# Two banks for the second layer's output columns of sample 0, and the products of the probabilities with v as bunches of eight

## The chip, the cores and the metric

The kernel runs on one core of a Trainium2 chip, as one program. The metric is the device time of one execution in microseconds; lower is better. TensorE (PE, with its weight loads PEld), VectorE (DVE), ScalarE (ACT), GpSimd (POOL) and the DMA queue on SyncE (SP) each work through their own list of instructions in order, and wait for one another through semaphores.

## The reference

A trunk of two layers is applied to two samples, each of 512 tokens by 1024 features, with the same weights. Layer 0 is RWKV-7 time mixing with a forward and a backward scan. Layer 1, where the change lies, is a two-dimensional neighbourhood attention over 8 rows by 64 columns of tokens, with 16 heads of 64 features, a gate and a projection; norms stand before and behind each layer:

```python
xn = _rms_norm(x, pre_norm_g[1])
proj = xn @ w_in + b_in
q, k, v, z = jnp.split(proj, 4, axis=-1)
o = _neighbourhood_attention(heads(q) * (HEAD_DIM ** -0.5), heads(k), heads(v), rpb)
h = (o.reshape(bsz, t, D_INNER) * jax.nn.silu(z)) @ w_o + b_o
x = x + _rms_norm(h, post_norm_g[1])
```

A query attends to all 8 rows and to a window of 16 columns. The scores get a bias and a mask, then a softmax, and the probabilities are multiplied with v.

## The kernel before

Activations lie with the features on the 128 partitions and the 512 tokens along the free dimension, so eight blocks k of 128 features make one sample. A projection column is one block p of 128 output features: 24 products of 128x128 by 128x512 into one PSUM bank, three for each k, since every fp32 operand is split into a high and a low part (`halves`, L375 the high, L376 the low) and high x high (L426), high x low (L427) and low x high (L428) are summed. The weights of a column come in two halves of 128x512, each loaded into `raw` (3 buffers) and split into `whi` and `wlo` (4 buffers each). The operands of a projection lie in pairs named `act` (18 buffers, nine pairs).

The first 1100 us are projections and scans whose order is written out by a planner; the change does not touch them. The rest of the program (`rest`) is written as interleaved generators: `run(g, (o, n))` takes n steps of o for each step of g. A scheduler then orders the instructions of each engine by its own estimate of times and by priorities: what stands under `high_priority(n)` is placed earlier where it can be. The stages of `rest` are:

- the last projections of sample 0 (`inproj(0)`) and the output projection of layer 0 for sample 1 (`out0(1)`), beside the attention of sample 0 (`heads(0, p)`, one call for each of the eight pairs of heads);
- the output columns of layer 1 for sample 0 (`out1(0)`), beside the normalisation of sample 1 between the layers (`norm0(1)`);
- the projections of sample 1 (`inproj(1)`, banks `pg`), beside the attention of sample 1 (`heads(1, p)`) and the transposes of `by_token`;
- the output projection of sample 1 (`last`).

In `heads`, a pair of heads is worked off in two half pairs of two column blocks n each, ns = (0, 1) and (2, 3). For a half pair come eight products q k into the bank `sc` (L1421, under priority SHP), then for each n the softmax on VectorE and ScalarE (L1430 to L1435), the transposes of the probabilities into `pt` (L1437), a copy to the factor `pts` (L1440), and after both n eight products with v into the bank `po` (L1450), four for each n: two parts e of the keys, two heads h, the heads on the two halves of the array's columns. At the end L1456 multiplies `po` with the gate into `oa`.

In `out1`, the operands are the eight `oa`, split by L375 and L376. Column p goes to the bank that OUT1[p % 4] names; ScalarE empties it at L1471 (out `os`) and squares it for the norm (L437, L440; sum L441). The bank `pm` is a single one, `pg` are two, which `inproj` and `out0` use in turn.

In `norm0`, after the sums of L452, a square root (L455), and the products of L464, the scale is copied out at L466. Then VectorE scales all eight blocks h (L1294), adds the loaded x (`xr`, 3 buffers, L1295), ScalarE squares (L1296, L1298) and VectorE sums (L1300). `x1n` makes the operands of `inproj(1)` from h (L1356 and L1357).

Of the kernel before, what the change touches and what calls it, by code (L numbers as in the profile page):

```python
# [234 lines left out]
class Trunk:  # L235
# [1 line left out]
    POST0, POST, POST2, POST3, NPA = 0.7, 1.0, 0.15, 0.66, 5  # L237
    HP, HS = (1000, 0), 1000
    SHP = 2000
    OUT1 = ("pm",) * 4  # L240
    LOW = 15
    LA = -40
    LATER = (0, 40, 0, 0)
# [1150 lines left out]
    def heads(self, s, p):  # L1394

        nc = self.nc
        vt, act, gps = nc.vector, nc.scalar, nc.gpsimd
        b = lambda tag, shape=(P, T), n=1, dt=F32: self.t(tag, shape, n, dt, self.ap)
        bias = b("bias", (P, 2, 3, 256), self.NBI)
        for h in range(2):  # L1400
            self.load(bias[:, h].rearrange("p a b -> p (a b)"), self.a["rpb"][2 * p + h])
        q, k, v = (self.load(b(kind, n=2), self.sp[kind, s, p]) for kind in ("q1", "k1", "v1"))
        yield
        vtok = b("vtok", (P, 7, P), self.NK)
        for j0, j1 in ((0, 4), (4, 7)):
            ps = self.p("pt", (P, 4, P))
            for j in range(j0, j1):
                nc.tensor.transpose(ps[:, j - j0], v[:, 64 * j:64 * j + P], self.ident)
            act.copy(vtok[:, j0:j1], ps[:, 0:j1 - j0])
            yield  # L1410
        op = self.p("po", (P, 4, P))
        cols = (0, 8, 24, 32)
        for ns in ((0, 1), (2, 3)):

            sc = self.p("sc", (P, 2, 2, 256))
            with self.tc.high_priority(self.SHP):
                for n in ns:
                    for a in (0, 64):
                        for h in range(2):
                            hs = slice(64 * h, 64 * h + 64)  # L1420
                            nc.tensor.matmul(  # L1421
                                sc[a:a + 64, h, n % 2], q[hs, n * P + a:n * P + a + 64], k[hs, 8 * cols[n]:8 * cols[n] + 256],
                                start=True, stop=True)
            pts = []
            for n in ns:
                pt = self.p("pt", (P, 2, 2, P))
                for h in range(2):
                    sb = b("sb", (P, 256), self.NSB)
                    mx = b("mx", (P, 4), 6)
                    vt.tensor_tensor_reduce(  # L1430
                        sb, sc[:, h, n % 2], bias[:, h, (0, 1, 1, 2)[n]], 1.0, -3.0e38, op0=ALU.add, op1=ALU.max, accum_out=mx[:, 0:1])
                    vt.tensor_scalar(mx[:, 1:2], mx[:, 0:1], -1.0, None, op0=ALU.mult)  # L1432
                    act.activation(sb, sb, AF.Exp, bias=mx[:, 1:2], accum_out=mx[:, 2:3])  # L1433
                    vt.reciprocal(mx[:, 3:4], mx[:, 2:3])
                    vt.tensor_scalar(sb, sb, mx[:, 3:4], None, op0=ALU.mult)  # L1435
                    for e in range(2):
                        nc.tensor.transpose(pt[:, h, e], sb[:, e * P:(e + 1) * P], self.ident)  # L1437
                    yield
                pts.append(b("pts", (P, 2, 2, P), self.NPT))
                act.copy(pts[-1], pt)  # L1440
                if n % 2 == 0:
                    yield
            if ns[1] == 3:
                while ("z1", s, p) not in self.sp:
                    yield
                z = self.load(b("z1"), self.sp["z1", s, p])
            for n in ns:
                for e in range(2):
                    for h in range(2):
                        nc.tensor.matmul(  # L1450
                            op[64 * h:64 * h + 64, n], vtok[:, cols[n] // 8 + 2 * e, 64 * h:64 * h + 64], pts[n % 2][:, h, e],
                            start=(e == 0), stop=(e == 1))
            yield
        with self.tc.high_priority(self.HP[s] if p == NP - 1 else 0):
            o = self.tmp() if s else self.t("oa", (P, T), NP, F32, self.ap)
            vt.tensor_tensor(o, op.rearrange("p n t -> p (n t)"), z, op=ALU.mult)  # L1456
            if s:
                lo, hi = (self.t("os", (P, T), 2 * NP, F32R, self.ap) for _ in range(2))
                o = self.halves(o, lo, hi)
        self.os[s].append(o)  # L1460
        yield

    def out1(self, s):
# [4 lines left out]
        for p in range(NP):  # L1468
            ps = yield from self.gemm(self.weight(self.a["w_ao"][p]), x, self.OUT1[p % 4])
            h = self.t("os", (P, T), 2 * NP, F32R, self.ap).bitcast(F32)  # L1470
# [419 lines left out]
```

## Time and profile before

| | |
|---|---|
| median of 3 runs | 1702.96 us (1696.2 to 1705.31) |
| profiled execution | 1697.02 us, its span 1695.2 us |
| mean granted TensorE clock in it | 0.959 |
| busy: PE, PEld | 1547.8 us (91%), 1178.6 us (70%) |
| busy: DVE, ACT | 1198.9 us (71%), 983.1 us (58%) |
| products with v (L1450) | 512 records, 1175.7 to 1655.5 us |
| scores (L1421) | 512 records, 1112.3 to 1629.5 us |
| eviction of an output column (L1471) | 8, median 682 ns, 1336.8 to 1394.6 us |

A row of a timeline reads: start, duration, engine, line, operation, out<-in, kind of tile, shape, count, and in brackets the idle time of the engine just before it and what ended that. Matmuls overlap in the array, so the distance between two starts is what a product costs, not its duration. A fp32 product with v or for scores has two records each. Times are from the span's start.

### The profile page before, as it was taken

The page shows a single profiled execution, that of the slowest core. Times are in us where ns is not written, and L with a number is a line of the kernel's source. Part 1 is how long each engine was busy: PE and PEld are TensorE (multiplying, and loading weights), DVE is VectorE, ACT ScalarE, POOL GpSimd, SP SyncE. Part 2 cuts the span into 40 slices and gives each one's busy share as a digit, 9 for nine tenths or more (in the row PEclk, how much of TensorE's full clock was granted, in tenths as well). Part 3 has the DMA queues.
Part 4 walks back from the last instruction along what each step waited for, and adds up shares of the span by engine and source line. Part 5 has one row for each costly group of instructions (what it writes and reads, how often), then busy time and mean ns, then how long its engine had stood idle before and what let it go on. Part 6 is the DMA issues. An engine that isn't in the chain of part 4 may idle for free.

```text
span 1695.2 us, 46252 instructions
## 1 busy us (share of the span) xinstructions
PE 1547.8 (91%) x18880; PEld 1178.6 (70%) x18880; DVE 1198.9 (71%) x2645; ACT 983.1 (58%) x2001; POOL 20.6 (1%) x64
## 2 busy tenths in 40 slices
PE   7989877987989898898899989999999889999997
PEld 6766655765756676676677767778777677777776
DVE  8986788777897888777798984534566746555564
ACT  5444665657767585567756545434566654555562
POOL 0000000000000000000000000000000000000000
PEclk9989888998998999899999999999999899999999
DMA  5435786778675777868674665464564237555553
GB/s 207 162 125 194 230 287 196 215 219 253 215 239 179 221 233 251 233 195 240 216 227 156 228 203 183 151 240 153 179 223 132 87 101 245 190 160 182 162 174 100
DMA packets 237365, 329.98 MB, mean 195 GB/s; under 512 B 53312, under 2 KB 118976, under 8 KB 237152
## 3 DMA queue, kind: packets, MB, share of 16 engines
q1 hardware_dynamic: 237152, 327.01, 60.7%
q8 instruction: 149, 2.44, 0.6%
q14 instruction: 64, 0.52, 0.1%
HBM read 223.52 MB, written 103.42 MB: 193 GB/s over the span
## 4 chain that ended last, share of the span: by engine, by line
PE 49%; DVE 9%; ACT 8%; DMA 6%; issue 3%; SPq 0%; DVEq 0%; ACTq 0%
PE pg L426 5%; PE pg L427 5%; PE pg L428 5%; PE pm L760 5%; PE pm L761 4%; PE pm L762 4%; DMA cab<-dab 3%; PE sc L1421 2%; PE pf L1077 2%; PE po L1450 2%; PE pt L1437 1%; PE zy L1123 1%; PE zy L1154 1%; PE pm L426 1%; DMA raw<-in_w_ao_dram 1%
## 5 line engine op out<-in xcount | busy, mean ns | idle before, releaser
L760 PE MATMUL pm<-act,whi 128*128 128x512 f32 x608 | 270.2, 444 | 19.7 <-ACT act L743 14.3
L761 PE MATMUL pm<-act,whi 128*128 128x512 f32 x608 | 247.8, 408 | 14.6 <-DVE act L745 14.3
L762 PE MATMUL pm<-act,wlo 128*128 128x512 f32 x608 | 246.0, 405 | 0.0
L376 DVE TENSOR_TENSOR wlo<-raw,whi 128x512 fp32r<-128x512 f32 x156 | 107.4, 690 | 96.8 <-ACT whi L375 88.8
L426 PE MATMUL pg<-act,whi 128*128 128x512 f32 x416 | 170.2, 410 | 1.9 <-DVE tmp L1377 1.9
L375 ACT CAST whi<-raw 128x512 fp32r<-128x512 f32 x156 | 96.4, 618 | 126.0 <-PE pg L427 51.5
L427 PE MATMUL pg<-act,whi 128*128 128x512 f32 x416 | 166.2, 400 | 0.0
L428 PE MATMUL pg<-act,wlo 128*128 128x512 f32 x416 | 164.3, 395 | 0.0
L760 PEld LDWEIGHTS pm<-act,whi 128*128 128x128 f32 x608 | 118.7, 195 | 62.4 <-ACT act L743 16.8
L761 PEld LDWEIGHTS pm<-act,whi 128*128 128x128 f32 x608 | 119.3, 196 | 41.7 <-DVE act L745 19.5
L723 DVE TENSOR_TENSOR wlo<-raw,whi 128x512 fp32r<-128x512 f32 x152 | 103.3, 687 | 54.0 <-ACT whi L721 53.8
L762 PEld LDWEIGHTS pm<-act,wlo 128*128 128x128 f32 x608 | 118.6, 195 | 27.7 <-DVE wlo L723 1.6
L721 ACT CAST whi<-raw 128x512 fp32r<-128x512 f32 x152 | 92.4, 618 | 72.4 <-PE pm L761 63.9
L426 PEld LDWEIGHTS pg<-act,whi 128*128 128x128 f32 x416 | 78.5, 189 | 19.1 <-DVE tmp L1377 2.7
L428 PEld LDWEIGHTS pg<-act,wlo 128*128 128x128 f32 x416 | 78.7, 189 | 16.7 <-issue 1.1
L427 PEld LDWEIGHTS pg<-act,whi 128*128 128x128 f32 x416 | 78.8, 189 | 15.1 <-issue 2.1
L967 DVE TENSOR_TENSOR N<-etmp,N 128x30 f32<-128x30 f32 (+14 forms) x240 | 79.8, 333 | 8.3
L1077 PE MATMUL pf<-cab 64*64 64x128 f32 (+1 forms) x2048 | 74.5, 278 | 12.2 <-issue 4.2
L966 DVE TENSOR_TENSOR etmp<-N 128x30 f32<-128x30 f32 (+14 forms) x240 | 78.4, 327 | 3.4
L1163 ACT COPY X<-zy 64x256 f32<-64x256 f32 x128 | 47.0, 367 | 50.0 <-PE zy L1154 42.3
L1433 ACT ACTIVATE sb<-sb,mx 128x256 f32<-128x256 f32 x128 | 64.0, 502 | 20.5 <-DVE mx L1432 19.9
L1077 PEld LDWEIGHTS pf<-cab 64*64 64x64 f32 x2048 | 60.1, 141 | 19.1 <-issue 9.9
(431 smaller groups left out, 3351.1 us busy)
## 6 DMA issues: line engine op xcount, KB each, us to landing
dab<-ab SPq DMA_DIRECT2D x32, 1024.0 KB
cab<-dab SPq DMA_DIRECT2D x64, 512.0 KB
raw<-in_w_in_dram SPq DMA_DIRECT2D x128, 256.0 KB
bias<-in_rpb_dram SPq DMA_DIRECT2D x32, 384.0 KB
raw<-in_w_z_dram SPq DMA_DIRECT2D x32, 256.0 KB
dz<-tmp SPq DMA_DIRECT2D x32, 256.0 KB
raw<-in_w_k_dram SPq DMA_DIRECT2D x32, 256.0 KB
dk<-tmp SPq DMA_DIRECT2D x32, 256.0 KB
```

Of the source, the lines that this page charges most:

```text
L375: self.nc.scalar.copy(hi, src)
L376: (eng or self.nc.vector).tensor_tensor(lo, src, hi.bitcast(F32), op=ALU.subtract)
L426: nc.tensor.matmul(ps, hi, x[k][0], start=(k == 0), stop=False)
L427: nc.tensor.matmul(ps, hi, x[k][1], start=False, stop=False)
L428: nc.tensor.matmul(ps, lo, x[k][0], start=False, stop=(k == KT - 1))
L721: nc.scalar.copy(hi, raw[h])
L723: nc.vector.tensor_tensor(lo, raw.pop(h), hi.bitcast(F32), op=ALU.subtract)
L760: nc.tensor.matmul(ps, hi[:, at], xh, start=(k == 0), stop=False)
L761: nc.tensor.matmul(ps, hi[:, at], xl, start=False, stop=False)
L762: nc.tensor.matmul(ps, lo[:, at], xh, start=False, stop=(k == KT - 1))
L967: vt.tensor_tensor(N[:, q + 1:, :q], tv, N[:, q + 1:, :q], op=ALU.add)
L1077: end = nc.tensor.matmul(f[half(1 - a), h, 0, d, g] if st.last else f[half(1 - a), h, :, d, g], ab[half(h), d, g, 2 * e[d] + a], rt if st. ...
```

## The change

The output columns of sample 0 go to `pm` and `pg` in turn. The eight products with v of a half pair are written under the priority of the scores, those of the later n first, and a dependence on TensorE alone holds the products of the earlier n behind them, so that the eight stand as one bunch. Nothing else is edited; lines behind the edit move down by six (L1471 becomes L1477), and L1450 becomes L1452.

```diff
-    OUT1 = ("pm",) * 4
+    OUT1 = ("pm", "pg", "pm", "pg")
...
-            for n in ns:
-                for e in range(2):
-                    for h in range(2):
-                        nc.tensor.matmul(
-                            op[64 * h:64 * h + 64, n], vtok[:, cols[n] // 8 + 2 * e, 64 * h:64 * h + 64], pts[n % 2][:, h, e],
-                            start=(e == 0), stop=(e == 1))
+            last = None
+            with self.tc.high_priority(self.SHP):
+                for n in reversed(ns):
+                    for e in range(2):
+                        for h in range(2):
+                            av = nc.tensor.matmul(
+                                op[64 * h:64 * h + 64, n], vtok[:, cols[n] // 8 + 2 * e, 64 * h:64 * h + 64], pts[n % 2][:, h, e],
+                                start=(e == 0), stop=(e == 1))
+                            if n % 2 == 0:
+                                self.behind(av, last)
+                            else:
+                                last = av
```

TensorE's order before, at the end of a pair of heads of sample 1 (`po_19806` is its bank, `pts_19966` and `pts_19999` the factors of n = 2 and 3, `sc_20126` the scores of the next pair, `pg_20031` a projection column):

```order
L426 MATMUL pg_20031<-act_18461,whi_20023 128x512
L427 MATMUL pg_20031<-act_18460,whi_20023 128x512
L428 MATMUL pg_20031<-act_18461,wlo_20024 128x512
L426 MATMUL pg_20031<-act_18465,whi_20023 128x512
L1450 MATMUL po_19806<-pts_19966,vtok_19785 64x128 x4
L1421 MATMUL sc_20126<-k_3624_20094,q_3623_20092 64x256 x8
L1450 MATMUL po_19806<-pts_19999,vtok_19785 64x128 x4
L427 MATMUL pg_20031<-act_18464,whi_20023 128x512
```

TensorE's order now, at the same bunch:

```order
L426 MATMUL pg_20031<-act_18477,whi_20027 128x512
L427 MATMUL pg_20031<-act_18476,whi_20027 128x512
L428 MATMUL pg_20031<-act_18477,wlo_20028 128x512
L426 MATMUL pg_20031<-act_18481,whi_20027 128x512
L1452 MATMUL po_19806<-pts_19999,vtok_19785 64x128 x4
L1452 MATMUL po_19806<-pts_19966,vtok_19785 64x128 x4
L1421 MATMUL sc_20126<-k_3624_20094,q_3623_20092 64x256 x8
L427 MATMUL pg_20031<-act_18480,whi_20027 128x512
```

The two fours now stand together, ahead of the scores instead of around them, and twelve projection products further back.

TensorE's order before, at the end of the last pair of heads of sample 0 (`po_17818`); `pm_18051` is the output column p=0, `pm_18104` p=1, `act_18035` and `act_18034` are the high and the low part of the last head pair's operand:

```order
L1450 MATMUL po_17818<-pts_17948,vtok_17787 64x128 x4
L1450 MATMUL po_17818<-pts_17978,vtok_17787 64x128 x4
L464 MATMUL pt_18117<-tmp_18087,ones 128x128 x4
L426 MATMUL pm_18051<-act_18035,whi_18047 128x512
L427 MATMUL pm_18051<-act_18034,whi_18047 128x512
L428 MATMUL pm_18051<-act_18035,wlo_18048 128x512
L426 MATMUL pm_18104<-act_18007,whi_18096 128x512
L427 MATMUL pm_18104<-act_18006,whi_18096 128x512
```

TensorE's order now, at the same place, where `pg_18104` is p=1 and `pg_18213` p=3:

```order
L1452 MATMUL po_17818<-pts_17978,vtok_17787 64x128 x4
L1452 MATMUL po_17818<-pts_17948,vtok_17787 64x128 x4
L464 MATMUL pt_18117<-tmp_18087,ones 128x128 x4
L426 MATMUL pm_18051<-act_18035,whi_18047 128x512
L426 MATMUL pg_18104<-act_18035,whi_18100 128x512
L427 MATMUL pm_18051<-act_18034,whi_18047 128x512
L428 MATMUL pm_18051<-act_18035,wlo_18048 128x512
L427 MATMUL pg_18104<-act_18034,whi_18100 128x512
L428 MATMUL pg_18104<-act_18035,wlo_18101 128x512
L426 MATMUL pg_18213<-act_18007,whi_18205 128x512
L427 MATMUL pg_18213<-act_18006,whi_18205 128x512
```

The first 21 products of p=1 have gone ahead of these rows, p=0 and p=1 end together, and the first half of p=3 (twelve products) follows ahead of p=2.

VectorE's order before, at the last head pair's `oa`, the low part of its operand (`act_18034`) and the normalisation's L1294 (h and hh are the eight blocks):

```order
L1456 TENSOR_TENSOR oa_17993<-po_17818,z_3117_17980 128x512
L376 TENSOR_TENSOR act_18034<-oa_17993,act_18035 128x512
L1294 SCALAR_TENSOR_TENSOR h_2934_17214<-h_2934_17214,cv,acc_17213 128x512
L1294 SCALAR_TENSOR_TENSOR h_2961_17326<-h_2961_17326,cv,acc_17213 128x512
L1294 SCALAR_TENSOR_TENSOR h_2987_17440<-h_2987_17440,cv,acc_17213 128x512
```

VectorE's order now, at the same place:

```order
L1462 TENSOR_TENSOR oa_17993<-po_17818,z_3117_17980 128x512
L1294 SCALAR_TENSOR_TENSOR h_2934_17214<-h_2934_17214,cv,acc_17213 128x512
L1294 SCALAR_TENSOR_TENSOR h_2961_17326<-h_2961_17326,cv,acc_17213 128x512
L1294 SCALAR_TENSOR_TENSOR h_2987_17440<-h_2987_17440,cv,acc_17213 128x512
L1294 SCALAR_TENSOR_TENSOR h_3015_17554<-h_3015_17554,cv,acc_17213 128x512
L1294 SCALAR_TENSOR_TENSOR hh_17668<-hh_17668,cv,acc_17213 128x512
L1294 SCALAR_TENSOR_TENSOR hh_17782<-hh_17782,cv,acc_17213 128x512
L1294 SCALAR_TENSOR_TENSOR hh_17896<-hh_17896,cv,acc_17213 128x512
L1294 SCALAR_TENSOR_TENSOR hh_18001<-hh_18001,cv,acc_17213 128x512
L376 TENSOR_TENSOR act_18034<-oa_17993,act_18035 128x512
L1295 TENSOR_TENSOR h_2934_17214<-h_2934_17214,xr_18141 128x512
```

The low part `act_18034` has moved behind all eight L1294.

## The prediction

> **What bounds the kernel now.** I read the page's first part, then the busy time by stretch, then the waits of the stretch in which TensorE is not full, and then that stretch instruction by instruction. Busy time by stretch (columns: stretch, its length, busy us and instructions of PE, PEld, DVE, ACT, POOL, then clock, DMA share, GB/s):
>
> ```profile
> 1240.00:1322.00 82.00, 82.00 (x575) 62.19 (x574) 53.89 (x188) 56.44 (x131) 0.00 (x0) 1.00 0.51 161
> 1334.00:1355.00 21.00, 16.56 (x52) 12.15 (x51) 15.60 (x25) 9.69 (x18) 0.00 (x0) 0.76 0.27 88
> 1355.00:1400.00 45.00, 39.43 (x172) 31.30 (x171) 21.73 (x37) 22.55 (x39) 0.00 (x0) 0.96 0.34 105
> 1428.00:1618.00 190.00, 189.50 (x1193) 143.83 (x1191) 107.53 (x375) 106.08 (x241) 0.00 (x0) 1.00 0.56 177
> ```
>
> The change lies in two kinds of stretch. While heads of the attention run beside projections (1240 to 1322, 1428 to 1618), TensorE is busy all the time: what is saved on TensorE there is time, what other engines do is not. In the output columns of sample 0 (1334 to 1400) TensorE has gaps and the granted clock falls to 0.76. The waits of 1322 to 1430 name the gap (engine, line, what it waited for: total, times, longest):
>
> ```profile
> PE pm L426 <- ACT os L1471: 9.2, 7, 2.8
> PE pg L426 <- DVE tmp L1377: 1.9, 1, 1.9
> ```
>
> All eight columns use the one `pm` bank, so each of the seven later ones waits until ScalarE has emptied it: 9.2 us. The timeline of TensorE there:
>
> ```profile
> 1321.64 0.40 PE L426 MATMUL pm<-act,whi 128*128 128x512 f32 x1
> ...
> 1328.21 1.88 PE L1437 MATMUL pt<-cc,sb 128*128 128x128 f32 x8 [0.36 <-DVE sb L1435]
> ...
> 1333.02 1.13 PE L464 MATMUL pt<-tmp,ones 128*128 128x128 f32 x8 [1.12 <-DVE tmp L460]
> 1334.77 0.49 PE L426 MATMUL pm<-act,whi 128*128 128x512 f32 x1 [0.61 <-ACT act L375]
> ...
> 1337.58 0.80 PE L426 MATMUL pm<-act,whi 128*128 128x512 f32 x1 [0.87 <-ACT os L1471]
> ...
> 1345.11 0.39 PE L428 MATMUL pm<-act,wlo 128*128 128x512 f32 x1
> 1348.22 0.50 PE L426 MATMUL pm<-act,whi 128*128 128x512 f32 x1 [2.72 <-ACT os L1471]
> ...
> 1349.40 0.63 PE L427 MATMUL pm<-act,whi 128*128 128x512 f32 x1
> 1349.83 0.63 PE L428 MATMUL pm<-act,wlo 128*128 128x512 f32 x1
> ...
> 1358.34 0.50 PE L426 MATMUL pm<-act,whi 128*128 128x512 f32 x1 [2.76 <-ACT os L1471]
> ...
> 1366.75 0.50 PE L426 MATMUL pm<-act,whi 128*128 128x512 f32 x1 [0.28 <-ACT os L1471]
> ...
> 1372.11 0.39 PE L428 MATMUL pm<-act,wlo 128*128 128x512 f32 x1
> 1373.57 0.50 PE L426 MATMUL pm<-act,whi 128*128 128x512 f32 x1 [1.07 <-ACT os L1471]
> ...
> 1393.46 0.40 PE L428 MATMUL pm<-act,wlo 128*128 128x512 f32 x1
> ```
>
> A column p=4 (24 products) takes from 1366.75 to 1372.11, and one step more: 5.5 us without a wait. After the wait of 2.72 us products start 0.43 us apart instead of 0.23 (1349.40, 1349.83): a gap also costs clock. From 1348.22 to the end of p=7 at 1393.7 there are six columns, 45.5 us for 33.0 us of products.
>
> **The change, part one: the output columns.** The order moves more than the bank. Since p=1 has a bank of its own, its first 21 products now stand before the products with v of the last head pair, and p=0's and p=1's last products stand together. I follow the changed order with the durations of the trace, taking 1321.64 as the same starting point. The other rows that I need, of ScalarE and VectorE:
>
> ```profile
> 1330.78 1.28 ACT L455 ACT_TABLE_LOAD   x1
> 1334.62 0.58 ACT L466 COPY acc<-pt 128x512 f32<-128x512 f32 x1
> 1345.31 0.62 ACT L375 CAST whi<-raw 128x512 fp32r<-128x512 f32 x1 [2.15 <-PE pm L427]
> 1345.83 0.62 ACT L1296 ACTIVATE xr<-h 128x512 f32<-128x512 f32 x1
> ...
> 1335.35 2.73 DVE L1294 SCALAR_TENSOR_TENSOR h<-h,cv,acc 128x512 f32<-128x512 f32 x4
> 1338.00 2.73 DVE L1294 SCALAR_TENSOR_TENSOR hh<-hh,cv,acc 128x512 f32<-128x512 f32 x4
> ...
> 1359.69 0.69 DVE L1300 TENSOR_TENSOR vs<-xr,vs 128x512 f32<-128x512 f32 x1
> ```
>
> (a) Up to the end of p=1. The 21 products (21 x 0.23 = 4.8 us) push the second half's transposes from 1328.21 to about 1332.7, since the wait of 0.36 us there and some slack are filled. L464 stood 4.8 us behind those transposes (the table load is within), so it comes at about 1337.5. The normalisation's scale, L466, now goes ahead of the cast of the last head, and ends at 1339.2. VectorE then does the eight L1294 (5.4 us, to 1344.7) and only behind them the L376 that makes the low half of the last head's operand, to 1345.4. Before, that L376 stood ahead of the eight. So TensorE, having done one L426 for each column, stands some six us at the first L427 with that half: the gap of the 0.87 us wait is closed, and a longer one opens. Four products later, p=0 and p=1 are done at about 1346.7; before, at 1345.4. Cost +1.3 us. Behind the waiting L427 in TensorE's queue stand p=3 and p=2, and nobody else waits for them yet.
>
> (b) The first half of p=3 stands next and needs a weight cast that ScalarE does behind L1296, L1298 and L1356 of the first block: L1295 at 1345.4 to 1346.1, three ScalarE steps to 1347.8, the cast to 1348.4. So six columns start at 1348.5, where before six started at 1348.22. They now cost 33.0 us, and 12 products at the low clock (12 x 0.2 = 2.4), the sums of L452 (0.9), and 0.7 for p=5's first weight, which waits for the last L1296 of the normalisation: 37.0 us, to 1385.5. Before it was 45.5 less 1.5 us of work that the order moves behind (L464 and three products of the next projection), 44.0. Gain 44.0 - 37.0 - 0.3 = 6.7 us; I take 7 for the whole of part one. The normalisation itself keeps its end near 1360.4: its VectorE part begins some 4 us later, but before, its first L1296 sat behind the cast that waited for TensorE until 1345.31, and that stall is gone.
>
> Bounds: if the six-us stop at L427 falls away, nothing but the columns counts, and 9.2 us of waits and some 3 us of clock go, 12. If the weight splits, behind the normalisation on VectorE, take all of it back, nothing. I stay nearer the middle since the order shows both stops. Of the 3 us of clock: the Trainium skill, "TensorE: Matmul & The Clock Gate", section "The HAM clock gate", has the clock halved only after an idle window of about 3.4 us. By that rule the waits of 2.7 us would cost no clock and the bound were 9.2. The trace disagrees: steps of 0.43 us follow the 2.72 us wait.
>
> (c) After p=7 the order of projection columns, transposes and L1478 is as before; the 1.9 us wait for L1377 stays.
>
> **Part two: the bunches.** From the timeline of TensorE, and in the last row the chain that ended last (each fp32 product with v has two records, so x8 is four products):
>
> ```profile
> 1507.14 0.39 PE L426 MATMUL pg<-act,whi 128*128 128x512 f32 x1
> 1507.46 0.66 PE L1450 MATMUL po<-pts,vtok 128*64 128x128 f32 x8
> 1508.06 1.09 PE L1421 MATMUL sc<-k,q 64*64 64x256 f32 x16
> 1509.08 0.66 PE L1450 MATMUL po<-pts,vtok 128*64 128x128 f32 x8
> 1509.67 0.50 PE L427 MATMUL pg<-act,whi 128*128 128x512 f32 x1
> 1510.00 0.39 PE L428 MATMUL pg<-act,wlo 128*128 128x512 f32 x1
> ...
> 1318.15 0.44 PE L1450 MATMUL po<-pts,vtok 128*64 128x128 f32 x4
> 1318.52 1.09 PE L1421 MATMUL sc<-k,q 64*64 64x256 f32 x16
> 1319.54 0.88 PE L1450 MATMUL po<-pts,vtok 128*64 128x128 f32 x12
> 1320.35 0.66 PE L1408 MATMUL pt<-cc,v 128*128 128x128 f32 x4
> ...
> 1471.38 1.02 PE po L1450 x16
> ```
>
> By starts, four records take 0.37, eight 0.60, twelve 0.81, sixteen 1.02: 0.215 for two products and 0.155 once per bunch. Going in and out of the full array costs 0.09 + 0.11 (0.32 and 0.33 between starts where 0.23 is the rule). Counted over TensorE's order: bunches fall from 58 to 32 (26 x 0.155 = 4.0), trips out of the full-array products from 54 to 42 (12 x 0.2 = 2.4), four uneven splits of three and five go (4 x 0.215 = 0.9), and three bunches of scores are now cut in two (3 x 0.6, about, = 1.8 back). Gain 5.5 us, nearly all where TensorE is full. Bounds 0 (another engine takes over) and 7.3 (the cut scores cost nothing).
>
> The new wait: a bunch begins with the later factor `pts` of its half pair and holds up the projection behind it. How long a factor takes, TensorE's transposes and ScalarE's copy:
>
> ```profile
> 1523.68 0.60 PE L1437 MATMUL pt<-cc,sb 128*128 128x128 f32 x4
> ...
> 1524.31 0.59 ACT L1440 COPY pts<-pt 128x512 f32<-128x512 f32 x1 [0.81 <-PE pt L1437]
> ```
>
> That is 1.2 us from the first transpose to the copied factor. Between a factor's last transpose and its bunch the changed order has over 4.2 us of other products everywhere but in the last head pair of sample 0, which is in (a). I cost the wait at nothing; the cover is those products.
>
> **Sum.** -7 - 5.5 = -12.5 us. The profiled execution took 1697.0 us (span 1695.2), six less than the median of 1703.0; the three runs spread from 1696.2 to 1705.3. The mean of the four is 1700.4, and I subtract from that: 1688.
>
> **Rivals.**
> 1. The bank is not the bound: the wait for ScalarE becomes a wait for weights, whose splits stand behind the normalisation's loads on VectorE. For it: the changed order puts p=5's weight behind the last L1296. Against: p=4 to p=7 waited in a time when VectorE was half idle. It takes the whole gain if the normalisation ends 8 us later, at 1368. Then only the bunches count: 1700.4 - 5.5 = 1695. The Trainium skill, same page, section "HAM oscillation", reports a kernel where PSUM double buffering "gave no further gain"; by that, this rival holds.
> 2. The bunches gain nothing, since the later scores hold up their softmax and TensorE waits there instead; for it, three groups of scores that are cut in two; against, some 8 us of other products between scores and transposes: 1693.
> 3. Slower: a bunch waits on TensorE for its later factor because ScalarE's copy stands behind weight casts. With 32 bunches it eats the 12.5 us at 0.4 us each, and at 0.7 us each the kernel is 10 us slower, 1710. For it: ScalarE runs in order, and its casts often wait for TensorE. Against: 31 bunches have over 4.2 us of cover for a copy that needs 1.2.
>
> That the change does not happen is no rival: the order shows 32 bunches of eight and the two banks.
>
> **Chances.** The forecast 0.60, rival 1 0.22, rival 2 0.12, rival 3 0.06. About 0.5% (8.5 us) is what a measurement of this kernel can tell from no change. Of the forecast's cases nine in ten are faster by more, rivals 1 and 2 lie mostly within: faster 0.62, same 0.31, slower 0.07. Range: 12 and 5.5 off the middle of the runs gives 1683, less 4 for the runs' spread, 1679; above, rivals 1 and 2 and the same spread, 1700. The forecast's own range is 1681 to 1694.
>
> **What would show it.** After the change: the group of waits of pm L426 for L1471 gone or under 2 us; a TensorE wait for VectorE's L376 of about 6 us near 1340 (shows (a)); p=7 ending 6 to 8 us sooner relative to L452; L1450's successor in 32 records groups of sixteen at 1.02 us; 1428 to 1618 shorter by about 3 us. I am wrong if TensorE waits for wlo or whi in the output columns for more than 5 us in all, or for `pts` in the bunches.

## The result, and the profile after

The changed kernel takes 1685.84 us in the median of five runs (1678.61 to 1689.01), beside 1702.96 us for the kernel before: a ratio of 0.9888, interval 0.9857 to 0.9918. Two later series gave 0.9887 (0.9853 to 0.9921) and 0.9904 (0.9873 to 0.9935). By these ratios the gain is 16 to 19 us; 12.5 were forecast. The profiled execution took 1685.84 us, its span is 1684.0 us. The page's first part has TensorE at 1537.9 us, 9.9 less than before.

The waits of TensorE from the last scores of sample 0 to the projections of sample 1 (1322 to 1430), and two of the stretches shown before:

```profile
PE pm L427 <- DVE act L376: 4.8, 1, 4.8
PE pg L426 <- DVE tmp L1377: 1.9, 1, 1.9
PE pm L426 <- ACT act L375: 1.2, 1, 1.2
PE pg L426 <- ACT whi L375: 1.0, 2, 0.8
```

```profile
1334.00:1355.00 21.00, 13.35 (x78) 9.70 (x77) 14.22 (x27) 9.99 (x19) 0.00 (x0) 0.76 0.21 69
1355.00:1400.00 45.00, 44.81 (x211) 37.05 (x210) 27.41 (x49) 25.36 (x44) 0.00 (x0) 1.00 0.41 128
```

The group of 9.2 us in seven waits for L1471 is gone. One stop of 4.8 us at L427 has come. Ahead of 1355 TensorE is idle for a third of the time; behind it, where it had 39.43 busy us of 45 and a clock of 0.96, it now has 44.81 and 1.00. The timeline of TensorE, with the first scores of the attention, the last group of sample 0 and the first of sample 1:

```profile
1118.92 1.09 PE L1421 MATMUL sc<-k,q 64*64 64x256 f32 x16
...
1323.47 0.88 PE L1421 MATMUL sc<-k,q 64*64 64x256 f32 x12
...
1337.79 1.05 PE L452 MATMUL pt<-ones,acc 128*128 128x1 f32 x8 [0.24 <-ACT pts L1440]
1340.48 1.13 PE L464 MATMUL pt<-tmp,ones 128*128 128x128 f32 x8 [0.62 <-DVE tmp L460]
1342.80 0.50 PE L426 MATMUL pm<-act,whi 128*128 128x512 f32 x1 [1.19 <-ACT act L375]
1348.31 0.80 PE L427 MATMUL pm<-act,whi 128*128 128x512 f32 x1 [4.78 <-DVE act L376]
1351.21 0.79 PE L426 MATMUL pg<-act,whi 128*128 128x512 f32 x1 [0.83 <-ACT whi L375]
...
1387.01 0.39 PE L428 MATMUL pg<-act,wlo 128*128 128x512 f32 x1
...
1426.26 1.09 PE L1421 MATMUL sc<-k,q 64*64 64x256 f32 x16
```

VectorE at the stop, and ScalarE at the wait of 0.83 us that follows it:

```profile
1342.27 2.74 DVE L1294 SCALAR_TENSOR_TENSOR h<-h,cv,acc 128x512 f32<-128x512 f32 x4 [0.74 <-ACT acc L466]
1344.92 2.73 DVE L1294 SCALAR_TENSOR_TENSOR hh<-hh,cv,acc 128x512 f32<-128x512 f32 x4
1347.57 0.68 DVE L376 TENSOR_TENSOR act<-oa,act 128x512 fp32r<-128x512 f32 x1
```

```profile
1348.89 0.63 ACT L1296 ACTIVATE xr<-h 128x512 f32<-128x512 f32 x1 [6.14 <-DVE h L1295]
...
1350.56 0.60 ACT L375 CAST whi<-raw 128x512 fp32r<-128x512 f32 x1
```

The low half is made behind the eight L1294, and p=3's weight is cast behind L1296: both as the order said.

For the comparison of kernels I cut each execution at three starts: A from the first scores of the attention to the last group of sample 0, B from there to the first scores of sample 1 (it holds the output columns), C from there to the end of the span. Before, these starts are 1112.33, 1318.52 and 1432.71; two of the rows:

```profile
1112.33 0.88 PE L1421 MATMUL sc<-k,q 64*64 64x256 f32 x12
...
1432.71 1.09 PE L1421 MATMUL sc<-k,q 64*64 64x256 f32 x16
```

| | A to end | A | B | C |
|---|---|---|---|---|
| before | 582.9 | 206.2 | 114.2 | 262.5 |
| after, first series | 565.1 | 204.5 | 102.8 | 257.7 |
| difference | -17.8 | -1.7 | -11.4 | -4.8 |

The scans ahead of A are the same code and took 6.6 us more in this execution of the changed kernel, which is spread between executions. The 17.8 us therefore stand beside a difference of 11.2 between the two spans, and agree with the 16 to 19 of the runs.

### The profile page after: what moved, and what is told of

It reads as the page before. It is cut to its first block, busy times and chain, and to the rows that moved or that the text cites. A ratio compares the mean times of both kernels' runs of the same rounds, so it can differ in the third digit from the quotient of the medians.

```text
span 1684.0 us, 46244 instructions
## 1 busy us (share of the span) xinstructions
PE 1537.9 (91%) x18880; PEld 1179.6 (70%) x18880; DVE 1199.0 (71%) x2645; ACT 982.6 (58%) x2001; POOL 20.7 (1%) x64
## 4 chain that ended last, share of the span: by engine, by line
PE 52%; DVE 9%; ACT 7%; DMA 5%; issue 3%; SPq 0%; DVEq 0%; ACTq 0%
PE pg L426 6%; PE pg L428 6%; PE pg L427 6%; PE pm L760 5%; PE pm L761 4%; PE pm L762 4%; DMA cab<-dab 2%; PE sc L1421 2%; PE po L1452 2%; PE pf L1077 2%; PE pt L1437 2%; PE zy L1123 1%; PE zy L1154 1%; PE us L1168 1%; ACT X L1163 1%
## 5 line engine op out<-in xcount | busy, mean ns | idle before, releaser
L426 PE MATMUL pg<-act,whi 128*128 128x512 f32 x448 | 182.1, 407 | 2.9 <-DVE tmp L1377 1.9
L427 PE MATMUL pg<-act,whi 128*128 128x512 f32 x448 | 178.1, 398 | 0.0
L428 PE MATMUL pg<-act,wlo 128*128 128x512 f32 x448 | 177.9, 398 | 0.0
L375 ACT CAST whi<-raw 128x512 fp32r<-128x512 f32 x156 | 96.3, 618 | 120.7 <-PE pg L427 61.7
L376 DVE TENSOR_TENSOR wlo<-raw,whi 128x512 fp32r<-128x512 f32 x156 | 107.2, 689 | 82.7 <-ACT whi L375 76.0
L760 PEld LDWEIGHTS pm<-act,whi 128*128 128x128 f32 x608 | 119.0, 196 | 64.1 <-ACT act L743 16.3
L426 PEld LDWEIGHTS pg<-act,whi 128*128 128x128 f32 x448 | 84.8, 189 | 20.9 <-DVE tmp L1377 2.4
L428 PEld LDWEIGHTS pg<-act,wlo 128*128 128x128 f32 x448 | 84.7, 189 | 19.8 <-issue 2.7
L427 PEld LDWEIGHTS pg<-act,whi 128*128 128x128 f32 x448 | 85.0, 190 | 17.1 <-issue 2.3
L1092 ACT COPY Tm<-pf 128x512 f32<-128x512 f32 x56 | 32.8, 586 | 66.7 <-DVE R L1085 66.2
```

Of the source, the lines that this page charges most:

```text
L375: self.nc.scalar.copy(hi, src)
L376: (eng or self.nc.vector).tensor_tensor(lo, src, hi.bitcast(F32), op=ALU.subtract)
L426: nc.tensor.matmul(ps, hi, x[k][0], start=(k == 0), stop=False)
L427: nc.tensor.matmul(ps, hi, x[k][1], start=False, stop=False)
L428: nc.tensor.matmul(ps, lo, x[k][0], start=False, stop=(k == KT - 1))
L760: nc.tensor.matmul(ps, hi[:, at], xh, start=(k == 0), stop=False)
```

## The experiments

The table has every profiled execution. "Waits" is the idle time of TensorE in B. "Slow steps" counts in B the pairs of projection products that start 0.36 us or more apart with no wait between, where 0.23 is the rule; each costs 0.2 us. In the rows with a star eleven products of a projection stand behind the mark between B and C instead of ahead of it: 2.5 us (11 x 0.23) are to be added to their B and taken off their C; "corrected" means this. In "dependence alone", besides, the mark between A and B stands ahead of twenty products (4.6 us) that are in A elsewhere, so that its B compares with no other row.

| kernel | ratio to before (interval) | A to end | B | waits | slow steps | C |
|---|---|---|---|---|---|---|
| before | | 582.9 | 114.2 | 13.4 | 34 | 262.5 |
| changed, three series | 0.9888, 0.9887, 0.9904 | 565.1, 567.0, 565.5 | 102.8, 105.0, 102.5 | 9.7, 9.5, 9.5 | 12, 25, 13 | 257.7, 257.4, 258.4 |
| banks alone | 0.9952 (0.9928 to 0.9977) | 573.5 | 104.0 | 9.5 | 14 | 263.3 |
| banks alone, again | 0.9937 (0.9909 to 0.9965) | 574.0 | 104.1 | 9.2 | 16 | 263.7 |
| bunches alone * | 0.9971 (0.9948 to 0.9994) | 576.4 | 111.2 | 17.0 | 19 | 260.6 |
| bunches alone, again * | 0.9976 (0.9953 to 1.0000) | 576.5 | 111.3 | 17.1 | 18 | 260.6 |
| low half first * | 0.9857 (0.9823 to 0.9891) | 558.4 | 93.3 | 3.9 | 10 | 260.6 |
| low half first, again * | 0.9860 (0.9829 to 0.9892) | 559.7 | 91.7 | 3.9 | 2 | 263.5 |
| three banks * | 0.9866 (0.9829 to 0.9902) | 560.7 | 91.5 | 4.3 | 0 | 264.7 |
| priority alone * | 0.9886 (0.9854 to 0.9917) | 563.1 | 93.5 | 3.2 | 12 | 264.1 |
| dependence alone * | 0.9907 (0.9875 to 0.9939) | 570.7 | 104.9 | 8.4 | 12 | 265.3 |
| banks, low half first * | 0.9909 (0.9873 to 0.9945) | 567.2 | 96.2 | 3.9 | 17 | 264.9 |

**The two parts apart.** Each was made alone, first in one series and then again beside the changed kernel.

```diff
 banks alone, against before:
-    OUT1 = ("pm",) * 4
+    OUT1 = ("pm", "pg", "pm", "pg")
 bunches alone, against the changed kernel:
-    OUT1 = ("pm", "pg", "pm", "pg")
+    OUT1 = ("pm",) * 4
```

> The kernel before with the two banks for the output columns alone; the products with v stay as they were (58 bunches, 54 trips out of the full-array products). Its order has the low half of the last head's operand behind the eight L1294, as the changed kernel has. Theory (the two parts add up, the banks are worth about 10 us): the seven waits for L1471 (9.2 us in all) are gone, one stop of about 4.8 us at L427 stands in their place, the column stage ends 9 to 11 us sooner; the time is 9 to 12 us below the kernel before (ratio 0.9930 to 0.9947), and the stretch from the first scores of sample 1 to the end keeps its 262.5 us within 0.5. Rival (the banks only move the wait to the weights, everything came from the bunches): the time stays within 3 us of the kernel before.

> The changed kernel with the single bank pm for all output columns, the bunches of eight kept (32 bunches, 40 trips; five more groups of scores are cut in two than in the changed kernel). Theory (the two parts add up): the stretch from the first scores of sample 1 to the end takes 257 to 258.5 us instead of 262.5, the part before the output columns gains 1 to 2 us, the waits for L1471 stand at 7 to 10 us; the time is 5 to 8 us below the kernel before (ratio 0.9953 to 0.9970). The stop at L427 for the low half stands here too, since the order has it behind the eight L1294, so some of this may be lost again in the column stage: no less than 2 us below. Rival (bunches gain nothing by themselves): within 2 us of the kernel before, the last stretch at 262 us or more.

Both rivals fall by the traces: the banks take 10 us from B and nothing from C (its 0.8 more than before is wait: 2.3 us of TensorE, before 1.5), the bunches 4.4 us from C, corrected. By the runs the banks bring 8.1 us (0.0048 of 1697), where 9 to 12 were expected, and the bunches 4.9, where 5 to 8 were. In the kernel with the bunches alone, TensorE's waits from 1325 to 1430 show the stop at L427 on top of the waits for the bank:

```profile
PE pm L426 <- ACT os L1477: 7.8, 7, 2.8
PE pm L427 <- DVE act L376: 4.9, 1, 4.9
```

So either part alone moves the low half behind the eight L1294, and both together do it once. The two gains come to 13 us, less than the 19 of the changed kernel. Timed a second time, it was expected at 13 to 18 us if the parts add up, and at 18 to 21 if they help one another; it came out at 19 (0.9887), as the rival had it. So the three were run side by side:

> The changed kernel once more, on one chip with the next three. Theory (the parts add up): its gain over the kernel before is the sum of the two parts measured beside it, within 3 us; by the traces so far 9.4 and 6.5, so some 16. Rival (they help one another): the gain is over 4 us more than the sum of the two.

> The two banks alone, a second time, beside the changed kernel. Theory: 9 to 10 us below the kernel before, 6 to 7 us above the changed kernel. Rival: 7 us or less below the kernel before, over 10 us above the changed kernel.

> The bunches of eight alone, a second time, beside the changed kernel. Theory: 5 to 7 us below the kernel before, 9 to 11 us above the changed kernel. Rival: 4 us or less below the kernel before, over 14 us above the changed kernel.

Here the changed kernel is 16.3 us below the kernel before, the parts 10.7 and 4.1: 14.8 in sum. That is within 3 us, so the sum holds for this series, though the intervals are wider than the difference from the rival; the bunches alone missed their 5 to 7 and are not told from no gain by the runs, while their trace repeats to 0.1 us. By the traces the parts come to 9.2 and 6.5, 15.7 in sum, and the changed kernel to 17.0 in the mean of three. Two terms are not additive and cancel in the traces: the waits in B (-4.0 and +3.7 for the parts, -3.8 for both), since the stop counts once, and the slow steps (-19 and -15 for the parts, -17 for both), since there are only 34. Whether the runs hold a real surplus of some 3 us above the sum stays open; the intervals are wider than that.

**The stop at L427.** One dependence on VectorE puts the eight L1294 behind the L376 of the last head's low half.

```diff
+        self.low = (eng or self.nc.vector).tensor_tensor(lo, src, hi.bitcast(F32), op=ALU.subtract)
...
+            ins = nc.vector.scalar_tensor_tensor(h, h, self.vec("post0", k), rstd, op0=ALU.mult, op1=ALU.mult)
+            self.behind(ins, self.os_low)
...
+        self.os_low = self.low
```

> The changed kernel with one dependence more on VectorE: the eight L1294 of the normalisation of sample 1 stand behind the L376 that makes the low half of the last head pair's operand. It takes away the stop of 4.8 us at L427. Theory (that stop hides work that is late anyhow: the weight cast for p=3 and the normalisation): of the 4.8 us at most 2 come back as time, the next wait is for whi or for the normalisation; time 0 to 2 us below the changed kernel. Rival (the stop is a plain cost on TensorE): 4 to 5 us below the changed kernel. Second rival (the normalisation now begins later and delays the projections of sample 1): 1 to 2 us above it.

> The changed kernel with the eight L1294 behind the low half of the last head's operand, a second time, now beside the changed kernel on one chip. Theory (the stop at L427 is a plain cost of 5.8 us of waits and some clock): 6 to 9 us below the changed kernel, ratio to the kernel before 0.983 to 0.987. Rival (the difference came from the two chips): within 2 us of the changed kernel.

> The kernel before with the two banks and with the eight L1294 behind the low half of the last head's operand; the products with v as they were (60 bunches, 53 trips). Theory (the stop at L427 is a cost of its own, 4.8 us of wait, the 0.8 us of the next wait and a us or more of low clock behind it): 6 to 8 us below the two banks alone, 15 to 18 us below the kernel before (ratio 0.989 to 0.991); the column stage has no wait for L376. Rival (that gain came only together with the bunches): within 2 us of the two banks alone, ratio 0.994 to 0.996.

My first theory, that the stop covers work that is late anyhow, fell. Beside the changed kernel this version has a median 6.7 us lower (1677.39 against 1684.10). In the mean of its executions B is 8.4 us shorter, corrected, and the way from A to the end 6.8: C gives 1.7 back, nearly all in the second execution, where TensorE waits 2.2 us for loads of k; the first has no such wait. VectorE and TensorE's waits (1325 to 1430), second execution:

```profile
1347.28 0.69 DVE L376 TENSOR_TENSOR act<-oa,act 128x512 fp32r<-128x512 f32 x1 [1.26 <-ACT act L375]
1347.88 2.73 DVE L1294 SCALAR_TENSOR_TENSOR h<-h,cv,acc 128x512 f32<-128x512 f32 x4
```

```profile
PE pg L426 <- DVE tmp L1378: 1.9, 1, 1.9
PE pm L426 <- ACT act L375: 1.2, 1, 1.2
PE pt L464 <- DVE tmp L460: 0.6, 1, 0.6
PE pt L452 <- ACT pts L1441: 0.2, 1, 0.2
```

There is no wait for L376 and none for a weight: p=3's cast now stands ahead of L1296. Of the 8.4 us 5.7 are waits (9.6 to 3.9) and 2.1 slow steps (17 to 6 in the mean). The same edit on the banks alone takes their gain from 9.4 us (the mean of two series) to 15.4 (a third) by the runs, and adds 6.5 us by the trace, so it doesn't need the bunches. The changed kernel with the low half first has the lowest ratios measured, 0.9857 and 0.9860. It has the better median and trace beside the changed kernel, but the two intervals of that series overlap (0.9873 to 0.9935, and 0.9829 to 0.9892): the traces show the gain, the runs alone don't.

**A third bank.**

```diff
-    OUT1 = ("pm", "pg", "pm", "pg")
+    OUT1 = ("pm", "pg", "pg")
...
-            ps = yield from self.gemm(self.weight(self.a["w_ao"][p]), x, self.OUT1[p % 4])
+            ps = yield from self.gemm(self.weight(self.a["w_ao"][p]), x, self.OUT1[p % 3])
```

> The changed kernel with three banks in turn (pm, pg, pg) for the output columns. Its order puts 21 products of p=2 ahead too, 19 of them ahead of the sums L452, and has the low half ahead of the L1294. Theory (two banks are enough, no wait for an eviction is left after the change): no gain from the third bank; the normalisation starts 3 to 4 us later, the stop at L427 goes; the time is within 2 us of the changed kernel. Rival (a column still waits for a bank): 4 us or more below it.

Its ratio (0.9866, of a series without the changed kernel) is lower than the changed kernel's three, though the intervals overlap, and from A to the end it takes 4.4 to 6.3 us less. So the rival's 4 us are there, but not for the rival's reason. Its order has the low half ahead of the L1294, so the stop at L427 is gone here too, and beside "low half first", which keeps two banks, it gains nothing in the runs (1672.84 against 1673.01 us). The theory that two banks are enough holds. That the gain from the stop would be taken back held at most in part: C is some 4 us longer than in the changed kernel, corrected, and TensorE waits 3.6 us there, 2.6 of it for loads of k. Whether the later normalisation causes these waits no run shows.

**Place or bunch.** Two versions take the bunch apart. The first keeps the priority without the reversed order and the dependence, the second the other way round.

```diff
 priority alone, against the changed kernel:
-                for n in reversed(ns):
+                for n in ns:
...
-                            if n % 2 == 0:
-                                self.behind(av, last)
-                            else:
-                                last = av
 dependence alone, against the changed kernel:
-            with self.tc.high_priority(self.SHP):
+            with self.tc.high_priority(0):
```

> The changed kernel with its priority for the products with v, but without the reversed order and without the dependence: half of the half pairs stand as two fours again (48 bunches, 53 trips, 36 groups of scores). Theory (it is the bunching that pays, not the earlier place): by the terms of the prediction ten bunches less than before save 1.6 us, the uneven splits 0.9, and the cut scores give back 1 to 3, so the stretch from the first scores of sample 1 to the end takes 260 to 262 us of TensorE work as before (less the waits and the twelve products that may cross the mark) and the time is 4 to 6 us above the changed kernel. Rival (the earlier place pays): within 1.5 us of the changed kernel, 258 us in that stretch.

> The changed kernel with the reversed order and the dependence, but without the priority: the products with v are scattered again, often as seven and one (49 bunches, 24 of them odd, 51 trips, 30 groups of scores, none cut). Theory (bunches and trips set the price, nothing else): nine bunches less than before save 1.4 us, three trips 0.6, and sixteen more odd bunches cost 1.7, so nothing is left of the gain of the bunches and the time is 5 to 7 us above the changed kernel, about that of the two banks alone. Rival (what pays is that no longer a softmax copy holds up the first four): within 2 us of the changed kernel.

By the time alone the rival of "priority alone" wins (0.9886 beside 0.9887 for the changed kernel in the same series), and "dependence alone" settles nothing (0.9907, some 3 us more, between its rival's 2 and its theory's 5). The stretch C says otherwise. From the first scores of sample 1 to a mark near the end, which holds the same last products, the busy time of TensorE (second number) and its instructions; before, changed, banks alone (again), bunches alone (again), priority alone, dependence alone:

```profile
1432.71:1690.00 257.29, 252.40 (x1527) 191.68 (x1526) 142.75 (x465) 134.43 (x307) 0.00 (x0) 1.00 0.51 160
```

```profile
1426.26:1680.00 253.74, 249.08 (x1527) 192.80 (x1526) 146.47 (x469) 133.58 (x307) 0.00 (x0) 1.00 0.52 166
```

```profile
1428.69:1690.00 261.31, 252.83 (x1527) 191.83 (x1526) 145.82 (x470) 134.35 (x307) 0.00 (x0) 0.99 0.51 163
```

```profile
1435.06:1694.00 258.94, 251.42 (x1538) 194.91 (x1537) 146.66 (x471) 135.03 (x308) 0.00 (x0) 0.99 0.53 167
```

```profile
1415.21:1678.00 262.79, 254.45 (x1538) 193.63 (x1537) 147.73 (x471) 135.16 (x308) 0.00 (x0) 0.99 0.51 164
```

```profile
1417.77:1683.00 265.23, 254.47 (x1538) 195.95 (x1537) 147.10 (x472) 134.69 (x309) 0.00 (x0) 0.99 0.52 165
```

With 2.5 us off where there are eleven instructions more, TensorE works 252.4 and 252.8 us without the bunches of eight, 249.1 and 248.9 with them, and 252.0 with the priority alone and with the dependence alone: either keeps 0.4 of 3.3 us. What saves the time of "priority alone" is its order: the low half stands ahead of the L1294 there.

```profile
1339.87 0.68 DVE L376 TENSOR_TENSOR act<-oa,act 128x512 fp32r<-128x512 f32 x1
1342.54 2.74 DVE L1294 SCALAR_TENSOR_TENSOR h<-h,cv,acc 128x512 f32<-128x512 f32 x4 [1.98 <-ACT acc L466]
```

It loses the 3 us of the bunches and is spared the stop. Against the version with the low half first, which also has no stop and does have the bunches, it is 3.4 to 4.7 us slower from A to the end. "Dependence alone" has the stop (5.1 us) and takes 3.7 to 5.6 us more than the changed kernel from A to the end, where 5 to 7 were expected for the time; its run interval doesn't tell that from nothing.

## Why the prediction was right, and where it was off

- **What bounds the kernel.** Right. The waits for L1471 were time (banks alone, 0.9952 and 0.9937), and TensorE's own work was time where it is full (C).
- **(a), the stop at L427.** The wait came where it was put, 4.78 us for "some six". The end of p=1 was to cost 1.3 us and cost nothing: L464 stands 17.0 us behind the last scores, before 14.5, so it comes 2.5 us later and not 4.5. Of the 2.0 between, some 0.8 is the marker alone: the bunch of twelve records that stood behind those scores stands ahead of them now.
- **(b), the six columns.** They took 36.0 us (1351.21 to 1387.24, one step behind the last row quoted), forecast 37.0, against 44.0 before: 8.0 gained. They start 27.7 us behind the last scores, before 29.7, where I had them 0.3 late. With 1.4 us more behind p=7 that makes the 11.4 of B; but these 1.4 are the slow steps behind the wait for L1377, which the second execution of the changed kernel has too, so they are chance (see the last section).
- **The term that was too small** is the clock. I counted "some 3 us", the steps behind the waits for L1471. The trace before has 34 slow steps in B, 6.8 us, with eleven ahead of p=2 and eight behind the wait for L1377; the changed kernel has 12, 25 and 13. I took 15 slow steps off and put 12 back in (b), 0.6 us net; with the banks alone 14 and 16 of the 34 are left, 3.6 to 4.0 us less. That is more than the 2 us by which their traces exceed my 7, but the eight behind L1377, 1.6 us of it, are chance of the one execution before. In place of my 7 for part one stand 8.1 and 10.7 by the runs, and 9.4 and 8.9 by the traces. My upper bound of 12, for the case that the stop falls away, was too low as well: with the low half first, the banks alone take 15.5 us from B, corrected, 9.5 of them waits and 3.4 clock.
- **Part two.** 5.5 us forecast; 4.9 and 4.1 by the runs, 6.5 and 6.4 by the traces, of which C gives 4.4. Of C's 4.8 us in the changed kernel 3.3 are TensorE's work, as forecast ("about 3"), and 1.5 are waits of the execution before (0.7 for L375, 0.5 for loads of k, 0.4 for L1435), which I had not counted. The first and the last stand also, at 0.9 to 1.0 and 0.4 to 0.7 us, in both executions of the banks alone; of the three of the changed kernel none has the first, and one has the last. So at least the wait for L375 belongs to the order of before and not to one execution; why it goes isn't shown. The price of a bunch and of a trip held: in C bunches fall from 28 to 16 and trips from 34 to 26, 12 x 0.155 + 8 x 0.2 = 3.5 us, less one group of scores that is cut.
- **The sum.** 12.5 forecast, 16 to 19 by the runs. I subtracted from 1700.4. In the first series the kernel before has a median of 1702.96, so the reference was 2.6 us low, and its medians give a gain of 17.1, so mine was 4.6 small. The two oppose each other, and that 1688 is so near 1685.84 is in part luck. In the three later series the kernel before has medians of 1695.0, 1697.7 and 1698.9. There the reference was high and both errors go the same way: the changed kernel's medians of 1679.0 and 1684.1 lie 9 and 4 us below the forecast, the first at the very end of its range.
- **Rival 1** (the weights become the bound) fell: all waits for whi make 1.0 us. **Rival 2** (bunches gain nothing) fell by the traces; by the runs alone only just in one series, and not in the other. **Rival 3** (bunches wait for their later factor) fell: no bunch of the changed kernel waits for `pts`; the one wait that ends with a `pts` copy, of 0.24 us, is that of the sums L452.
- **What would show it.** "p=7 sooner relative to L452" was a poor mark: 21 products of p=1 now stand ahead of L452, so the distance fell by 14 us. The last scores, which the change leaves nearly in place, were the better one.

## What to carry to other kernels

When a change moves work between queues, look in the new order for the operand whose producer has fallen behind a block of unrelated work, and put that producer first: here one such dependence on VectorE brought some 7 us by the traces on top of the 16 to 19. Price a wait on TensorE with the slow steps behind it, and count them all over the stage, not only behind the waits that are removed; and look at several executions, since the same wait can cost 1.6 us of clock or nothing. Where a variant comes out at the same total, compare stretches before drawing a conclusion: "priority alone" equals the changed kernel with two differences that cancel.

## What the runs showed of the hardware

The clock behind a wait does not go by the length of the wait alone. The same wait for L1377, 1.87 us here and 1.86 to 1.96 in all, is followed by seven or eight slow steps in seven of the fourteen profiled executions and by none in the other seven, within the same program too. The changed kernel, first series, and again:

```profile
1411.08 0.50 PE L426 MATMUL pg<-act,whi 128*128 128x512 f32 x1 [1.87 <-DVE tmp L1377]
1411.42 0.40 PE L427 MATMUL pg<-act,whi 128*128 128x512 f32 x1
1411.65 0.39 PE L428 MATMUL pg<-act,wlo 128*128 128x512 f32 x1
1411.88 0.40 PE L426 MATMUL pg<-act,whi 128*128 128x512 f32 x1
```

```profile
1409.18 0.53 PE L426 MATMUL pg<-act,whi 128*128 128x512 f32 x1 [1.87 <-DVE tmp L1377]
1409.52 0.62 PE L427 MATMUL pg<-act,whi 128*128 128x512 f32 x1
1409.94 0.63 PE L428 MATMUL pg<-act,wlo 128*128 128x512 f32 x1
1410.37 0.63 PE L426 MATMUL pg<-act,whi 128*128 128x512 f32 x1
```

In the second the distance between starts goes from 0.23 to 0.43 us, up to 1412.93, for 1.6 us in all; with the other five slow steps more, this is about the difference between B of 102.8 and of 105.0 in one program.

What decides is where the wait falls. In the clock records of all fourteen traces every stretch at one granted clock, 1.00 or 0.50, but the last, which the record cuts off, lasts a multiple of 3.41 us: the clock changes only on a raster of 3.41 us, and the raster lies otherwise in each execution. The steps of the raster around this wait, in the changed kernel again, in its first series, and in the banks alone again (columns: stretch, its length, busy us and instructions of PE, then clock, DMA share, GB/s):

```profile
1406.10:1409.51 3.41, 1.54 (x11) 1.00 0.93 351
1409.51:1412.92 3.41, 3.41 (x9) 0.50 1.00 293
```

```profile
1406.45:1409.86 3.41, 2.76 (x20) 1.00 0.49 184
1409.86:1413.27 3.41, 2.19 (x10) 1.00 1.00 329
```

```profile
1410.06:1413.47 3.41, 1.58 (x12) 1.00 0.83 312
1413.47:1416.88 3.41, 3.38 (x15) 1.00 1.01 297
```

In the first the whole wait lies within one step, which leaves TensorE 1.54 us busy there, and the step behind it runs at half the clock. In the second the wait is parted by an end of a step, and in the third all but 0.03 us lies in one step: the clock stays. So it is in all fourteen: the seven executions in which the wait lies whole in one step, with 1.54 to 1.55 us busy, are those with the slow steps, and the other seven have 1.58 us or more in each step. This holds for this wait between projection products. Ahead of the columns, among sums and transposes, the clock also fell behind steps that were busy for 0.68 of their length ("priority alone") and 0.75 ("banks, low half first"), so no limit for the busy share in general is shown.

The Trainium skill, "TensorE: Matmul & The Clock Gate", section "The HAM clock gate", calls the activity window free-running, so that where work falls in it differs from run to run. The traces agree with that: same wait, both outcomes. The same section asks for an idle window of about 3.4 us before the clock falls. The traces disagree, as they did for the 2.72 us wait in the prediction: 1.87 us were enough where they fell whole into one step.
